# Turning 32 x 128 gather indices: one index load and VectorE squares in place of a column load and a TensorE product

## Chip, cores, metric

One core of one Trainium2 chip. The metric is device time in microseconds (us) of one execution; medians are over several executions, and the ratios compare fast executions with fast ones (an execution counts as slow here when it is over 1.5% above the fastest of the same kernel).

## The reference

```python
def setup_inputs():
    batch, seq, dim = 32, 512, 1024
    x = np.random.randn(batch, seq, dim).astype(np.float32)
    indices = np.random.randint(0, seq, (batch, 128)).astype(np.int32)

def reference(x, indices):          # x [32, 512, 1024], indices [32, 128]
    for b in range(batch):
        result[b] = x[b, indices[b]]   # 128 rows of 4 KB for each batch
```

16.8 MB are written. 15.2 MB of rows are read by the count of the gathers' queue, because from batch 5 on the kernel fetches each distinct row only once. (The page's own line for HBM says 16.81 MB read; why the two differ was not looked into.)

## The kernel before

A gather (indirect transfer, issued by GpSimd) wants one index per partition, so the 32 x 128 table of indices must be turned into 128 x 32. The first five batches (HEAD) are gathered straight into output blocks and stored. For the later 27, VectorE and TensorE first find the distinct rows, GpSimd fetches only these, and TensorE spreads them to the 128 places. Eight buffers (a ring) hold fetched rows. Stores go out on the SyncE queue. The parts that matter here:

```python
first = const.tile([N, 1], indices.dtype, name="first")          # batch 0 as a column
nc.sync.dma_start(out=first[:], in_=indices.rearrange("b n -> n b")[:, 0:1])
vals = const.tile([B, N], indices.dtype, name="vals")            # all indices, by batch
nc.sync.dma_start(out=vals[:], in_=indices)
# ... GpSimd builds small tables: diff, rank (8 pieces), shift ...
dve(v.memset, vf[:], 0.0)
dve(v.tensor_copy, out=vf[:B], in_=<low words of vals>)          # fp16
pe(mm, tr[:], lhsT=vf[:], rhs=ident[:], start=True, stop=True)   # TensorE turns them
dve(v.tensor_copy, out=idxT[:], in_=tr[:])
dve(v.tensor_copy, out=idxF[:], in_=tr[:])
# ... near likewise, from tr ...
for b in range(HEAD):
    gather(blocks[b], first[:].bitcast(I32)[:, 0:1] if b == 0 else idxT[:, b:b + 1], b)
    store(b)
# ... grouping, fetching and spreading of batches 5 to 31 ...
```

Of the kernel before, what the change touches and what calls it, by code (L numbers as in the profile page):

```python
# [6 lines left out]
F32 = mybir.dt.float32  # L7
F16 = mybir.dt.float16
I32 = mybir.dt.int32
ALU = mybir.AluOpType  # L10
# [18 lines left out]
def kernel(ctx, tc, x, indices, out):  # L29
# [14 lines left out]
    nc = tc.nc  # L44
    B, S, D = x.shape
    N = indices.shape[1]
    HEAD, RING, FAR = 5, 8, 1024
    assert S <= FAR
    const = ctx.enter_context(tc.tile_pool(name="const", bufs=1))
# [6 lines left out]
    psm = ctx.enter_context(tc.tile_pool(name="psm", bufs=1, space=PS))  # L56
    pout = ctx.enter_context(tc.tile_pool(name="pout", bufs=3, space=PS))
    pe, dve = InOrder(tc), InOrder(tc)
    mm, v = nc.tensor.matmul, nc.vector


    first = const.tile([N, 1], indices.dtype, name="first")
    nc.sync.dma_start(out=first[:], in_=indices.rearrange("b n -> n b")[:, 0:1])
    vals = const.tile([B, N], indices.dtype, name="vals")
    nc.sync.dma_start(out=vals[:], in_=indices)

# [4 lines left out]
    for e in range(8):  # L71
# [11 lines left out]
    ident = const.tile([N, B], F16, name="ident")  # L83
# [6 lines left out]
    dve(v.tensor_copy, out=turn[:], in_=rank[:].rearrange("p e q -> p (e q)"))  # L90
    vf = const.tile([N, N], F16, name="vf")
    dve(v.memset, vf[:], 0.0)
    dve(v.tensor_copy, out=vf[:B],
        in_=vals[:].bitcast(I32).rearrange("p (n two) -> p n two", two=2)[:, :, 0])


    tr = psm.tile([N, B], F32, name="pos")
    pe(mm, tr[:], lhsT=vf[:], rhs=ident[:], start=True, stop=True)
    idxT = const.tile([N, B], I32, name="idxT")
    dve(v.tensor_copy, out=idxT[:], in_=tr[:])  # L100
    idxF = const.tile([N, B], F32, name="idxF")
    dve(v.tensor_copy, out=idxF[:], in_=tr[:])
    near = const.tile([N, B], F16, name="near")
    dve(v.tensor_scalar, out=near[:], in0=tr[:], scalar1=float(-FAR), scalar2=None, op0=ALU.add)

    xf = x.flatten_outer_dims()
    of = out.flatten_outer_dims()
# [1 line left out]
    def gather(dst, at, b, **kw):  # L109
        nc.gpsimd.indirect_dma_start(  # L110
            out=dst[:], out_offset=None,
            in_=xf[:], in_offset=bass.IndirectOffsetOnAxis(ap=at, axis=0),
            element_offset=b * S * D, **kw)

    def store(b):
        nc.sync.dma_start(out=of[b * N:(b + 1) * N], in_=blocks[b][:])

    blocks = [rows.tile([N, D], F32, name=f"block{b}") for b in range(B)]
    for b in range(HEAD):
        gather(blocks[b], first[:].bitcast(I32)[:, 0:1] if b == 0 else idxT[:, b:b + 1], b)  # L120
        store(b)

    def table(name, dtype):
# [148 lines left out]
```

## Time and profile before

| | before |
|---|---|
| median of the first three executions | 89.02 us (88.86 to 89.25) |
| span of the profiled execution | 87.5 us (that execution: 89.52 us, slower than the median) |
| bytes moved in the whole run | 32.11 MB |
| transfer rate on the plateau, 12 to 84 us | 418 GB/s |
| first gather issued | 2.79 us |
| second gather issued | 4.68 us |

The page cuts the span in 40 slices. The "GB/s" row says how fast transfers moved in each, and it is the row to read first: it is flat at about 418 from slice 7 on, and only the start (the ramp) is lower. The timeline has one line for each instruction: start, length, engine, source line, operation, output<-input, and in brackets how long the engine had been idle and what ended that. The lines themselves stand in the prediction.

### The profile page before, as it was taken

The numbers are of one execution on the slowest core, as the hardware profiler recorded it, in microseconds if no ns is written. First come the engines' busy times: TensorE is split into PE (matmuls) and PEld (weight loads), VectorE is DVE, ScalarE is ACT, GpSimd is POOL, SyncE is SP. The second block draws the span as 40 slices with busy tenths as digits, with TensorE's granted clock in tenths as the row PEclk, the third lists the DMA queues.
The fourth block names the chain that finished last, engine by engine and source line by source line (L and its number), as shares of the span: only waits on it lengthen the run. The fifth ranks groups of instructions, "written<-read, shape, count | busy, mean of one in ns | idle before, by whom it ended". The sixth has DMA issues, their size and how long they took to land.

```text
span 87.5 us, 931 instructions
## 1 busy us (share of the span) xinstructions
PE 58.3 (67%) x184; PEld 23.8 (27%) x184; DVE 41.8 (48%) x265; ACT 40.5 (46%) x63; POOL 33.6 (38%) x46
## 2 busy tenths in 40 slices
PE   0141302006999999999999999998878888885000
PEld 0121101003334343434343433333333332221000
DVE  2399944520497979797979797862000000000000
ACT  6999400000365655555565655554544445555000
POOL 7677787780054545454544444444400000000000
PEclk9999999999999999999999999999999999999995
DMA  0088999999999999999999999999999999999960
GB/s 0 15 223 200 257 352 403 419 419 419 419 416 418 419 421 419 418 418 418 419 414 418 418 412 419 418 418 419 418 419 419 418 419 419 419 419 419 419 251 6
DMA packets 9413, 32.11 MB, mean 367 GB/s; under 512 B 1559, under 2 KB 1591, under 8 KB 9408
## 3 DMA queue, kind: packets, MB, share of 16 engines
q1 hardware_dynamic: 4800, 16.81, 47.2%
q0 software_dynamic: 4608, 15.24, 45.5%
q14 instruction: 4, 0.03, 0.1%
q8 instruction: 1, 0.02, 0.1%
HBM read 16.81 MB, written 16.78 MB: 384 GB/s over the span
## 4 chain that ended last, share of the span: by engine, by line
PE 29%; DVE 29%; DMA 22%; issue 5%; another core or an unknown queue 4%; POOL 1%; ACT 1%; SPq 0%; POOLq 0%; DVEq 0%
PE ps L24 25%; DMA u<-in_x_dram,at 19%; DVE junk L24 5%; DVE s L24 3%; DVE pack L24 3%; DVE s L207 3%; DMA vals<-in_indices_dram 3%; DVE junk L188 3%; DVE lead L24 2%; DVE nth L24 2%; PE pos L24 2%; DVE slot L24 2%; DVE pack L200 1%; DVE atF L204 1%
## 5 line engine op out<-in xcount | busy, mean ns | idle before, releaser
L24 PE MATMUL ps<-u,s 128*128 128x512 f32 x108 | 53.9, 626 | 3.6 <-DMA u<-in_x_dram,at 3.6
L226 ACT COPY block<-ps 128x512 f32<-128x512 f32 x54 | 31.6, 585 | 39.4 <-PE ps L24 31.1
L110 POOL DMA_INDIRECT u<-in_x_dram,at x27 | 26.9, 997 | 26.2 <-PE rk L24 13.0
L24 PEld LDWEIGHTS ps<-u,s 128*128 128x128 f32 x108 | 18.8, 194 | 29.1 <-issue 16.0
L24 DVE SCALAR_TENSOR_TENSOR junk<-bc,idxF,below 128x128 f16<-128x128 f32 x18 | 6.3, 350 | 3.3 <-PE rk L24 3.3
L218 ACT COPY u<-zero 128x1024 f32<-128x1024 f32 x8 | 7.7, 1040 | 0.0
L24 DVE TENSOR_SCALAR s<-bc,atF 128x128 f32<-128x128 f32 x18 | 6.3, 351 | 0.6
L24 PE MATMUL rk<-lead,above 128*128 128x1 f16 x18 | 2.9, 163 | 5.2 <-DVE junk L24 5.2
L24 DVE TENSOR_SCALAR lead<-cnt 128x1 f16<-128x1 f32 (+1 forms) x36 | 3.9, 150 | 4.6 <-remote 4.1
L24 DVE TENSOR_SCALAR pack<-turn,slot,lead 128x128 f16<-128x128 f16 x18 | 5.7, 315 | 0.7
L202 PE MATMUL pos<-near,pack 128*128 128x1 f16 x9 | 1.4, 181 | 5.9 <-DVE pack L200 4.3
L110 POOL DMA_INDIRECT block<-in_x_dram,idxT x4 | 3.8, 946 | 1.7 <-issue 0.9
L24 PEld LDWEIGHTS <-pack 128*128 128x128 f16 x18 | 1.7, 96 | 9.2 <-DVE pack L24 8.8
L24 PE MATMUL bc<-vf,ident 128*128 128x128 f16 x18 | 3.9, 227 | 0.0
L24 PE MATMUL pos<-near,pack 128*128 128x1 f16 x18 | 3.1, 172 | 0.9
L202 PEld LDWEIGHTS <-pack 128*128 128x128 f16 x9 | 0.8, 104 | 9.0 <-DVE pack L200 4.4
L200 DVE TENSOR_SCALAR pack<-turn,slot,lead 128x128 f16<-128x128 f16 x9 | 2.3, 320 | 2.0 <-remote 2.0
L24 DVE TENSOR_TENSOR nth<-nth,shift 128x1 int32<-128x1 int32 x18 | 2.9, 159 | 0.6
L24 DVE CAST slot<-nth 128x1 f32<-128x1 int32 x18 | 2.8, 154 | 0.6
L24 DVE TENSOR_SCALAR at<-pos 128x1 int32<-128x1 f32 x18 | 2.7, 149 | 0.8 <-PE pos L24 0.5
L207 DVE TENSOR_SCALAR s<-bc,atF 128x128 f32<-128x128 f32 x9 | 2.6, 345 | 0.9 <-DVE atF L204 0.9
L188 DVE SCALAR_TENSOR_TENSOR junk<-bc,idxF,below 128x128 f16<-128x128 f32 x9 | 3.0, 345 | 0.0
(37 smaller groups left out, 24.0 us busy)
## 6 DMA issues: line engine op xcount, KB each, us to landing
out_dram<-block SPq DMA_DIRECT2D x32, 512.0 KB
u<-in_x_dram,at POOLq DMA_INDIRECT x27
block<-in_x_dram,idxT POOLq DMA_INDIRECT x4
vals<-in_indices_dram SPq DMA_DIRECT2D x1, 32.0 KB
first<-in_indices_dram SPq DMA_DIRECT2D x1, 1.0 KB
block<-in_x_dram,first POOLq DMA_INDIRECT x1
```

The costliest lines, as they stand in the source:

```text
L24: self.last = do(*args, **kw)
L110: nc.gpsimd.indirect_dma_start(out=dst[:], out_offset=None, in_=xf[:], in_offset=bass.IndirectOffsetOnAxis(ap=at, axis=0), element_offset= ...
L188: v.scalar_tensor_tensor(out=junk[:], in0=bc[:, b - g0], scalar=idxF[:, col(b)], in1=below[:], op0=ALU.is_equal, op1=ALU.mult, accum_out=c ...
L200: v.tensor_scalar(out=pack[:], in0=turn[:], scalar1=slot[:, col(b)], scalar2=lead[:, col(b)], op0=ALU.is_equal, op1=ALU.mult)
L202: pe.last = mm(pos[:, b - g0:b - g0 + 1], lhsT=pack[:], rhs=near[:, col(b)], start=True, stop=True)
L204: v.tensor_scalar(out=t[:, w], in0=pos[:, :n], scalar1=float(FAR), scalar2=None, op0=ALU.add)
L207: dve.last = v.tensor_scalar(out=s[:], in0=bc[:, b - g0], scalar1=atF[:, col(b)], scalar2=None, op0=ALU.is_equal)
L218: nc.scalar.copy(out=u[:], in_=zero[:].to_broadcast([N, D]))
L226: nc.scalar.copy(out=blocks[b][:, w], in_=ps[:])
```

## The change

Its intent: load the indices once only, and let VectorE turn them in four squares of 32 x 32. The small column load with its 128 packets goes, so does the TensorE product. The price is that gather 0 no longer has indices of its own and must wait for the turned ones.

```diff
-    first = const.tile([N, 1], indices.dtype, name="first")
-    nc.sync.dma_start(out=first[:], in_=indices.rearrange("b n -> n b")[:, 0:1])
     vals = const.tile([B, N], indices.dtype, name="vals")
     nc.sync.dma_start(out=vals[:], in_=indices)
 ...
-    dve(v.tensor_copy, out=vf[:B],
-        in_=vals[:].bitcast(I32).rearrange("p (n two) -> p n two", two=2)[:, :, 0])
-    tr = psm.tile([N, B], F32, name="pos")
-    pe(mm, tr[:], lhsT=vf[:], rhs=ident[:], start=True, stop=True)
+    low = vals[:].bitcast(I32).rearrange("p (n two) -> p n two", two=2)[:, :, 0]
     idxT = const.tile([N, B], I32, name="idxT")
-    dve(v.tensor_copy, out=idxT[:], in_=tr[:])
+    for n in range(0, N, B):
+        dve(v.transpose, out=idxT[n:n + B], in_=low[:, n:n + B])
+    dve(v.tensor_copy, out=vf[:B], in_=low)
 ... (idxF and near now read idxT instead of tr)
-        gather(blocks[b], first[:].bitcast(I32)[:, 0:1] if b == 0 else idxT[:, b:b + 1], b)
+        gather(blocks[b], idxT[:, b:b + 1], b)
```

More of the change, by code (lines that the diff above doesn't have):

```diff
@@ L92 @@
     dve(v.memset, vf[:], 0.0)
-    dve(v.tensor_copy, out=vf[:B],
-        in_=vals[:].bitcast(I32).rearrange("p (n two) -> p n two", two=2)[:, :, 0])
-    tr = psm.tile([N, B], F32, name="pos")
-    pe(mm, tr[:], lhsT=vf[:], rhs=ident[:], start=True, stop=True)
+    low = vals[:].bitcast(I32).rearrange("p (n two) -> p n two", two=2)[:, :, 0]
     idxT = const.tile([N, B], I32, name="idxT")
-    dve(v.tensor_copy, out=idxT[:], in_=tr[:])
+    for n in range(0, N, B):
+        dve(v.transpose, out=idxT[n:n + B], in_=low[:, n:n + B])
+    dve(v.tensor_copy, out=vf[:B], in_=low)
     idxF = const.tile([N, B], F32, name="idxF")
-    dve(v.tensor_copy, out=idxF[:], in_=tr[:])
+    dve(v.tensor_copy, out=idxF[:], in_=idxT[:])
     near = const.tile([N, B], F16, name="near")
-    dve(v.tensor_scalar, out=near[:], in0=tr[:], scalar1=float(-FAR), scalar2=None, op0=ALU.add)
+    dve(v.tensor_scalar, out=near[:], in0=idxT[:], scalar1=float(-FAR), scalar2=None, op0=ALU.add)
     xf = x.flatten_outer_dims()
```

## The prediction

> **What bounds the kernel now.** I read the page first: the busy shares, the 40 slices, the DMA queues. Busiest of the engines is TensorE, and none is full; the DMA rows decide it.
>
> ```profile
> PE 58.3 (67%) x184; PEld 23.8 (27%) x184; DVE 41.8 (48%) x265; ACT 40.5 (46%) x63; POOL 33.6 (38%) x46
> ...
> DMA  0088999999999999999999999999999999999960
> GB/s 0 15 223 200 257 352 403 419 419 419 419 416 418 419 421 419 418 418 418 419 414 418 418 412 419 418 418 419 418 419 419 418 419 419 419 419 419 419 251 6
> ...
> HBM read 16.81 MB, written 16.78 MB: 384 GB/s over the span
> ```
>
> One slice is 87.5 / 40 = 2.19 us. From slice 7 (15 us) to slice 38 (83 us) the transfers run at 412 to 421 GB/s without a gap: a plateau, and the kernel is bound by bytes. Only the ramp in slices 1 to 6 is below it. The DMA view of the window from 12 to 84 us says how flat the plateau is:
>
> ```profile
> DMA packets 8667, 30.06 MB, mean 418 GB/s; under 512 B 1336, under 2 KB 1336, under 8 KB 8662
> ```
>
> So 32.11 - 30.06 = about 2 MB of the run's 32.11 MB moves outside these 72 us, some 1.8 MB of it before 12 us. Everything after the ramp is a matter of bytes over 418 GB/s, and the change alters hardly any bytes. What the change can move is the ramp. The chain of waits names TensorE at 29% and VectorE at 29%; I set it aside for the end time, because TensorE's matmuls repeat every 2.07 us a batch (two batches in the 4.13 us from 24.02 to 28.16 us of the chain), whereas a batch's bytes, about 27 gathers' share of (15.24 - 5 x 0.524) / 27 = 0.467 MB plus a store of 0.524 MB, need 0.991 / 0.418 = 2.37 us. TensorE runs ahead and then waits for transfers.
>
> Next the timeline from 0 to 22 us, for GpSimd (start, length, instruction, idle time before it):
>
> ```profile
> 2.27 0.15 POOL L78 IOTA shift<- 128x32 int32 x1
> 2.79 1.11 POOL L110 DMA_INDIRECT block<-in_x_dram,first  x1 [0.37 <-DMA first<-in_indices_dram]
> 4.68 0.95 POOL L110 DMA_INDIRECT block<-in_x_dram,idxT  x1 [0.79 <-DVE idxF L24]
> 5.93 0.95 POOL L110 DMA_INDIRECT block<-in_x_dram,idxT  x1 [0.30 <-issue]
> ```
>
> The gathers are issued one after another, 0.95 to 1.00 us each and 0.30 us between. From the second to the thirteenth (18.80 us) none waits for data by more than this. So the start of the second gather fixes the twelve that fill the ramp; the first stands alone, 1.89 us ahead of it. Now what these two starts wait for, in the same timeline:
>
> ```profile
> 0.74 0.38 SPq L63 DMA_DIRECT2D first<-in_indices_dram  x1
> 1.18 0.41 SPq L65 DMA_DIRECT2D vals<-in_indices_dram  x1
> ...
> 2.52 0.11 DVE L24 MEMSET vf<- 128x64 uint32 x1
> ...
> 3.64 0.27 DVE L24 CAST vf<-vals 32x128 f16<-32x128 int32 x1 [1.00 <-DMA vals<-in_indices_dram]
> ...
> 3.97 0.21 PE L21 MATMUL pos<-ident,vf 128*128 128x32 f16 x1 [3.97 <-DVE vf L24]
> ...
> 4.21 0.19 DVE L24 CAST idxT<-pos 128x32 int32<-128x32 f32 x1 [0.30 <-PE pos L21]
> 4.32 0.18 DVE L24 COPY idxF<-pos 128x32 f32<-128x32 f32 x1
> ```
>
> The wide index load is issued second and lands at 3.54 us (the chain gives it 2.36 us from 1.18). Then cast, product, copy: 3.64 to 4.40 us. GpSimd starts 0.28 us after.
>
> **What the skill says.** "VectorE: DVE Perf Modes", section "The three transpose paths": VectorE turns blocks of 32x32 only. This is why the 32x128 indices need four instructions. The trace of before has no such instruction. The same page, "Two Vector instructions with no wait between them": an instruction whose output starts in another quadrant of 32 partitions than the last one's is held until all earlier ones have finished. The four squares go to four quadrants, so three of them should be held. In before, 128x32 operations last 0.18 to 0.19 us and unheld ones start 0.10 to 0.11 us apart (idxT, idxF), so holding would double their cost. "DMA: Bandwidth & Descriptors", section "Anatomy of one DMA — SWDGE (gpsimd) path": about 2.0 us are fixed, however few the bytes. It agrees in size: vals, 32 KB, takes 2.36 us to land. The same page, "Specifications", puts the fabric ceiling at 435 GB/s; the plateau of 418 lies just under it, so there is no reserve to catch up a late start.
>
> **The change, part by part.**
> - Removed: the column load `first`. It had let gather 0 start at 2.79 us. It was issued before vals, so vals now goes out at 0.74 instead of 1.18, 0.44 us earlier. Its 128 tiny packets are no bytes to speak of.
> - Removed from the path to idxT: cast (0.33 us to the product's start), product and its wait (0.24), copy (0.19): 3.64 to 4.40, 0.76 us.
> - Added to it: four squares. Unheld: 3 x 0.10 + 0.19 = 0.49 us; held: 4 x 0.19 = 0.76 us, or 0.95 if a square costs 0.24. I choose 0.70.
> - Start of the squares: with the old latency vals is ready at 3.64 - 0.44 = 3.20 us. If it was slow only because it queued behind `first`, it could be ready when the memset ends, 2.63 us. I choose 3.05.
> - Moved: cast of vf now comes after the squares; products for the comparisons start about 4.0 us as before, idxF and near come from SBUF. VectorE's rank work starts within 0.3 us of its old 4.62. It has slack: `at` of the first group is written at 7.77 and first used at 9.68 us.
>
> Sum: idxT at 3.05 + 0.70 = 3.75, gather 0 at 4.03 us, which is 1.24 later than 2.79. The first gather took 1.11 us against 0.95 for the next; I let it stay so, and gather 1 starts at 4.03 + 1.11 + 0.30 = 5.44, which is 0.76 later than 4.68. All gathers up to the thirteenth move by that. The order of instructions in the changed kernel confirms it: five gathers by idxT in a row, the first waiting for VectorE.
>
> To the end: if the whole ramp moves by 0.76 us, so does the end. If the slow part of the ramp ends at a fixed time (the rate reaches 401 GB/s at 12 us, just when VectorE's first burst ends at 11.96), the loss is the bytes moved in the last 0.76 us before, about 0.76 x 300 GB/s = 0.23 MB, over 418 = 0.55 us. I take **+0.6 us**: 89.02 + 0.6 = 89.6 us.
>
> **The rivals.**
> - *An index path that is quicker than the old one.* vals ready at 2.65 and unheld squares 0.49: idxT at 3.14, gather 0 at 3.42, gather 1 at 4.83, only 0.15 later than before. Then 89.0 to 89.2. For it: the packets of vals move mostly from 2.2 to 2.6 us, and only a last trace of 10 GB/s at 3.2 to 3.3 us keeps it from landing. Against: that straggler may come again.
> - *A slow path.* Squares of 0.24 us held, strided source, vals at 3.20: gather 1 1.16 us later, 90.1. Also, idxF and near now read SBUF while GpSimd writes the first descriptors, and might hold it for some tenths.
> - *The ramp is hidden anyway.* Gather 0 moved slowly and alone (its store could be issued only at 7.48 us), so bunching it with gather 1 may lose nothing, and the end moves by 0.3 or less. Against: a plateau with no reserve never repays a late byte.
> - *TensorE becomes the bound.* Its first spreading product at 20.44 us follows a VectorE stall of 1.7 to 2.3 us which the profile gives to an unknown queue. By 20 us thirteen gathers and five stores (8.9 MB) are asked for and some 5.2 MB moved, so 3.7 MB or 9 us of transfers are waiting: a stall would have to grow by many us. Unlikely.
>
> **Range and chances.** The paths above give +0.0 to +1.1 us; runs of before spread by 0.2 us either way. So 88.9 to 90.3 should hold it 8 times in 10. The lines for 2% are 87.2 and 90.8 us. Faster needs something outside this account, as no part of the path to the end shrinks by 1.8 us: 1%. Slower needs a delay of 1.8 us in the ramp or a transfer gap: 4%. Within: 95%.
>
> **What would show it.** Right: the plateau stays at 418 GB/s; vals issued at 0.74 and landed by 3.1; four squares of about 0.2 us; the first gather about 4.0 and the second about 5.4 us, then 1.25 to 1.30 apart; the first store near 8.5 instead of 7.48; the end about 0.6 later. Wrong in its steps: vals landing still at 3.5 (issue order bought nothing), squares far from 0.2 us, or a second gather later than 0.76 with an end that does not move. Wrong altogether: the plateau changes rate, or a gap opens in it.

## The result

The changed kernel is slightly slower: 90.12 us median (89.68 to 90.38, 4 executions) against 88.95 (88.86 to 89.25, 4 executions). The ratio is 1.0121, 95% interval 1.0071 to 1.017. A ratio here is the mean time of one kernel's fast runs over that of the other's fast runs of the same rounds, so it is not quite the ratio of the medians. Two more measurements followed (below): 1.005 (1.0016 to 1.0083) and 1.0111 (1.0064 to 1.0158). The mean of the three ratios is 1.0094, which is 0.0094 x 89.0 = 0.84 us. This is real, but under the 2% line, and inside the predicted range.

The page of the changed kernel, the rows of transfers in 40 slices of 2.2 us:

```profile
DMA  0048879999999999999999999999999999999950
GB/s 15 0 85 309 297 244 420 418 416 418 420 418 422 420 418 416 418 415 422 416 413 407 416 416 422 418 420 420 416 418 420 416 418 416 420 424 416 424 229 7
```

The plateau is the same as before (about 418 GB/s); the ramp is what differs. Here is what the ramp starts with, from the timeline of SyncE's queue, of VectorE and of GpSimd:

```profile
0.74 0.39 SPq L63 DMA_DIRECT2D vals<-in_indices_dram  x1
...
2.52 0.11 DVE L24 MEMSET vf<- 128x64 uint32 x1
2.55 0.79 DVE L24 STREAM_TRANSPOSE idxT<-vals 32x32 int32<-32x32 int32 x4
3.37 0.21 DVE L24 CAST vf<-vals 32x128 f16<-32x128 int32 x1
3.52 0.16 DVE L24 CAST idxF<-idxT 128x32 f32<-128x32 int32 x1
...
3.62 1.11 POOL L107 DMA_INDIRECT block<-in_x_dram,idxT  x1 [1.20 <-DVE vf L24]
5.04 0.95 POOL L107 DMA_INDIRECT block<-in_x_dram,idxT  x1 [0.31 <-issue]
6.29 0.94 POOL L107 DMA_INDIRECT block<-in_x_dram,idxT  x1 [0.30 <-issue]
```

The squares start as soon as VectorE is free, take 0.79 us together, and the first gather is issued at 3.62 instead of 2.79 us (+0.83), the second at 5.04 instead of 4.68 (+0.36). The bracket at the first gather names "DVE vf", an instruction that started at 3.37, when the last square had ended; the indices that it needs are those of the squares.

Now the same stretch as bytes. Each line below is one microsecond; the last two columns are the busy share of the 16 DMA engines and the rate in GB/s. Before:

```profile
6.00:7.00 1.00, 0.00 (x0) 0.00 (x0) 1.00 (x10) 1.00 (x2) 0.88 (x1) 1.00 1.03 274
7.00:8.00 1.00, 0.42 (x3) 0.29 (x4) 1.00 (x9) 1.00 (x2) 0.82 (x1) 1.00 0.53 119
8.00:9.00 1.00, 0.00 (x0) 0.00 (x0) 1.00 (x7) 1.00 (x2) 0.69 (x2) 1.00 1.09 311
9.00:10.00 1.00, 0.50 (x4) 0.25 (x3) 1.00 (x7) 0.69 (x1) 0.70 (x2) 1.00 0.93 291
10.00:11.00 1.00, 0.33 (x2) 0.17 (x2) 0.79 (x7) 0.00 (x0) 0.69 (x2) 1.00 0.94 221
11.00:12.00 1.00, 0.00 (x0) 0.00 (x0) 0.96 (x5) 0.00 (x0) 0.99 (x1) 1.00 0.86 291
12.00:13.00 1.00, 0.00 (x0) 0.00 (x0) 0.00 (x0) 0.00 (x0) 0.71 (x1) 1.00 1.01 414
```

Changed:

```profile
6.00:7.00 1.00, 0.28 (x3) 0.20 (x4) 1.00 (x10) 1.00 (x2) 0.71 (x1) 1.00 0.76 283
7.00:8.00 1.00, 0.15 (x2) 0.09 (x3) 1.00 (x9) 1.00 (x2) 0.70 (x2) 1.00 0.89 270
8.00:9.00 1.00, 0.23 (x2) 0.07 (x1) 1.00 (x9) 1.00 (x2) 0.69 (x2) 1.00 0.83 303
9.00:10.00 1.00, 0.67 (x4) 0.34 (x4) 0.76 (x4) 0.69 (x1) 0.74 (x1) 1.00 1.04 348
10.00:11.00 1.00, 0.00 (x0) 0.00 (x0) 0.97 (x6) 0.00 (x0) 0.96 (x1) 1.00 0.68 238
11.00:12.00 1.00, 0.09 (x1) 0.10 (x1) 0.96 (x6) 0.00 (x0) 0.70 (x2) 1.00 0.56 123
12.00:13.00 1.00, 0.71 (x5) 0.38 (x6) 0.68 (x5) 0.00 (x0) 0.70 (x2) 1.00 0.88 319
```

One microsecond at 1 GB/s is 0.001 MB, so the last column sums directly. In this pair of profiles the changed kernel moves 1.20 MB against 1.00 MB from 6 to 10 us, the mean rate from 0 to 10 us is 132 GB/s in both, and it falls behind between 11 and 13 us, where it moves 0.44 MB against 0.71. But the two are level at 10 us only because the profile of before has a late second gather (4.68 us). Three kernels that take as long as before and issue it at 4.18 to 4.31 us (column load with squares, short gap, stores exchanged; all below) had moved 1.50 to 1.57 MB by 10 us in their profiles; the changed kernel had moved 1.30 to 1.32 MB in its three. Against these the debt is there by 10 us already. By 16 us the pair shows a debt too. The DMA view of the first 16 us, before and then changed:

```profile
DMA packets 1116, 3.47 MB, mean 217 GB/s; under 512 B 246, under 2 KB 278, under 8 KB 1115
```

```profile
DMA packets 915, 3.26 MB, mean 204 GB/s; under 512 B 96, under 2 KB 128, under 8 KB 914
```

The debt is 0.21 MB; at 418 GB/s that is 0.5 us, and the plateau never repays it. The spans of the two profiles differ by 0.6 us (88.1 and 87.5).

### The profile page after: what moved, and what is told of

It is laid out like the page before. It is cut to its first block, busy times and chain, and to the rows that moved or that the text cites. A ratio compares the mean times of both kernels' runs of the same rounds, so it can differ in the third digit from the quotient of the medians.

```text
span 88.1 us, 929 instructions
## 1 busy us (share of the span) xinstructions
PE 59.1 (67%) x183; PEld 24.3 (28%) x183; DVE 42.4 (48%) x268; ACT 40.6 (46%) x63; POOL 33.6 (38%) x46
## 4 chain that ended last, share of the span: by engine, by line
DMA 47%; PE 19%; DVE 16%; issue 6%; POOL 3%; ACT 1%; POOLq 0%
DMA u<-in_x_dram,at 47%; PE ps L24 17%; DVE junk L24 2%; DVE junk L185 2%; DVE s L24 2%; DVE pack L24 2%; POOL block L107 2%; POOL rank L74 1%; DVE nth L24 1%; DVE lead L24 1%; DVE slot L24 1%; PE pos L24 1%; DVE idxT L24 1%; ACT block L223 1%; DVE lead L188 1%
## 5 line engine op out<-in xcount | busy, mean ns | idle before, releaser
L24 DVE TENSOR_SCALAR s<-bc,atF 128x128 f32<-128x128 f32 x18 | 6.3, 351 | 0.6
L24 DVE TENSOR_SCALAR pack<-turn,slot,lead 128x128 f16<-128x128 f16 x18 | 5.7, 314 | 0.7
L107 POOL DMA_INDIRECT block<-in_x_dram,idxT x5 | 4.9, 979 | 2.4 <-DVE vf L24 1.2
L24 PE MATMUL bc<-vf,ident 128*128 128x128 f16 x18 | 3.9, 227 | 0.0
L182 PE MATMUL bc<-vf,ident 128*128 128x128 f16 x9 | 1.1, 309 | 3.6 <-DVE vf L24 3.6
L24 PEld LDWEIGHTS <-ident 128*128 128x128 f16 x18 | 1.8, 102 | 4.1 <-issue 4.1
```

The costliest lines, as they stand in the source:

```text
L24: self.last = do(*args, **kw)
L107: nc.gpsimd.indirect_dma_start(out=dst[:], out_offset=None, in_=xf[:], in_offset=bass.IndirectOffsetOnAxis(ap=at, axis=0), element_offset= ...
L182: mm(bc[:, b - g0], lhsT=ident[:, col(b)].to_broadcast([N, N]), rhs=vf[:], start=True, stop=True)
```

## The experiments

Three theories went in. **Second gather:** the end follows the start of the second gather and of the train behind it. **First gather:** the end follows the first gather, since the gathers' queue is then busy for so long that the second has time to spare. **Squares:** the VectorE path itself costs. Later came **first store:** the ramp is slow because only gathers run, and ends when stores begin. In the table, "MB by 16 us" and the issue times are from one profile of each kernel, the ratio from five rounds against the kernel before; the first row is the one profile that this document has of the kernel before. The medians take in slow executions where there were some (one each of "gather 0 later" and "store 1 ahead", three of the last row); the ratios do not.

| kernel | first, second gather issued (us) | MB by 16 us | median us | ratio (95% interval) |
|---|---|---|---|---|
| before | 2.79, 4.68 | 3.47 | 89.0 to 89.15 | 1 |
| changed, second measurement | 3.63, 5.04 | 3.19 | 89.65 | 1.005 (1.0016 to 1.0083) |
| changed, third measurement | 3.78, 5.21 | 3.26 | 89.88 | 1.0111 (1.0064 to 1.0158) |
| squares, column load kept | 2.76, 4.18 | 3.66 | 89.10 | 0.9987 (0.9952 to 1.0023) |
| product, column load gone | 3.66, 5.07 | 3.27 | 89.92 | 1.0074 (1.004 to 1.0108) |
| before, long gap behind gather 0 | 2.76, 6.29 | 3.07 | 90.27 | 1.0144 (1.0108 to 1.0179) |
| before, short gap | 2.76, 4.31 | 3.52 | 89.13 | 0.9994 (0.9947 to 1.0042) |
| before, middle gap | 2.76, 4.74 | 3.45 | 89.40 | 1.0032 (0.9988 to 1.0076) |
| before, gather 0 a little late | 3.10, 4.52 | 3.55 | 89.21 | 1.0039 (0.9992 to 1.0086) |
| before, gather 0 later | 3.94, 5.38 | 3.14 | 90.26 | 1.0103 (1.0053 to 1.0153) |
| before, store 1 ahead of store 0 | 2.83, 4.31 | 3.45 | 89.28 | 1.0016 (0.9962 to 1.007) |
| before, gather 0 in two halves | 3.30, 4.67 (the halves) | 3.05 | 90.07 | 1.0107 (1.0051 to 1.0163) |
| column, squares, tables later | 2.76, 4.16 | 3.38 | 90.05 | 1.0041 (0.9996 to 1.0085) |

Read downward: the kernels with 3.27 MB or less by 16 us have ratios of 1.005 to 1.0144, those with 3.38 MB or more 0.9987 to 1.0041. One profile stands beside several timed executions, so this is a regularity over twelve kernels, not a law for one.

### The change again, as a yardstick

No edit. 

> The changed kernel itself, beside the kernel before in five rounds on one chip, as the yardstick for the other runs. The first measurement gave a ratio of 1.012 with an interval of 1.007 to 1.017; I expect 1.008 to 1.015, the first gather issued at 3.6 us and the second at 5.0.

Measured 1.005; a third time:

> The changed kernel once more, as the yardstick of this call: the first two measurements gave ratios of 1.012 and 1.005, whose intervals meet at 1.007 to 1.008. I expect 1.004 to 1.011.

Measured 1.0111. The squares start at 2.55 or 2.65 us, the first gather at 3.63 or 3.78. The size of the loss is thus known as 0.5 to 1.2% and no better.

### Undo one half: column load back, squares kept

```diff
 (changed kernel)
+    first = const.tile([N, 1], indices.dtype, name="first")
+    nc.sync.dma_start(out=first[:], in_=indices.rearrange("b n -> n b")[:, 0:1])
     vals = ...
-        gather(blocks[b], idxT[:, b:b + 1], b)
+        gather(blocks[b], first[:].bitcast(I32)[:, 0:1] if b == 0 else idxT[:, b:b + 1], b)
```

> The squares stay, the column load of batch 0 comes back ahead of the wide load, so that the first gather is again issued at 2.79 us. Theory 'first gather or first store' (what the change costs is the later first gather): back to the kernel before, ratio 0.998 to 1.003. Theory 'second gather' (the end follows the start of the second gather and the train behind it; with the wide load again second, the squares end at 4.4 us or so, second gather near 4.7 as before): also about 1.000. Theory 'squares' (the VectorE path itself costs, by locks or order): stays near 1.010.

Measured 0.9987. The loss is gone, with all four squares still there. "Squares" falls: VectorE's squares cost nothing at the end of the kernel. They gain nothing either, though 3.66 MB by 16 us is the best of all; the interval of the time includes 1. The squares had to wait for vals, which landed 1.67 us after its issue although the column load was ahead of it (before: 2.36 us):

```profile
2.88 0.85 DVE L24 STREAM_TRANSPOSE idxT<-vals 32x32 int32<-32x32 int32 x4 [0.24 <-DMA vals<-in_indices_dram]
```

### Undo the other half: product kept, column load gone

```diff
 (kernel before)
-    first = const.tile([N, 1], indices.dtype, name="first")
-    nc.sync.dma_start(out=first[:], in_=indices.rearrange("b n -> n b")[:, 0:1])
-        gather(blocks[b], first[:].bitcast(I32)[:, 0:1] if b == 0 else idxT[:, b:b + 1], b)
+        gather(blocks[b], idxT[:, b:b + 1], b)
```

> The column load is taken away, TensorE still turns the indices. The wide load lands at 2.5 us, cast, product and copy take 0.76, the first gather is issued at about 3.6 us, the second 1.41 later. Theory 'first gather or first store': like the changed kernel, ratio 1.008 to 1.015. Theory 'second gather' (+0.3 us): 1.003 to 1.004. Theory 'squares': 1.000.

Measured 1.0074, with the start of the gathers almost that of the changed kernel:

```profile
3.66 1.11 POOL L108 DMA_INDIRECT block<-in_x_dram,idxT  x1 [1.24 <-DVE idxF L24]
5.07 0.95 POOL L108 DMA_INDIRECT block<-in_x_dram,idxT  x1 [0.30 <-issue]
```

With the run above this settles which part of the change costs: taking away the column load does, and how the indices are turned does not. The intervals of the two runs do not touch.

### Move the second gather alone: a long gap

```diff
 (kernel before)
+    idle = const.tile([N, 1700], I32, name="idle")
+    pool = InOrder(tc)
     for b in range(HEAD):
+        if b == 1:
+            pool(nc.gpsimd.iota, idle[:], pattern=[[1, 1700]], base=0, channel_multiplier=0)
-        gather(...)
+        pool(gather, ...)
```

> The kernel before, with one dummy GpSimd operation of about 1 us between the first and the second gather: the first stays at 2.79 us, the second and all behind it start 0.3 to 0.6 us later. Theory 'second gather': the end moves by as much, ratio 1.003 to 1.007. Theory 'first gather': [...]a second gather issued at 5.1 us has 0.3 us to spare or so and the ratio stays 0.998 to 1.002.

Measured 1.0144, and not for either reason: the dummy was longer than meant (1.56 us), and VectorE's cast was held as well. Timeline of GpSimd and VectorE:

```profile
3.88 1.56 POOL L24 IOTA idle<- 128x1700 int32 x1
6.29 0.95 POOL L110 DMA_INDIRECT block<-in_x_dram,idxT  x1 [0.85 <-DVE idxF L24]
...
3.24 2.28 DVE L24 CAST vf<-vals 32x128 f16<-32x128 int32 x1 [0.60 <-DMA vals<-in_indices_dram]
```

The cast of 0.2 to 0.3 us lasted 2.28 us and ended at 5.52, 0.08 after the dummy. The Trainium skill says this: "SBUF — State Buffer", section "SBUF: two separate sides", calls the port pair that VectorE and GpSimd share "an **exclusive lock**, not a bandwidth split"; whichever starts first holds it for its whole instruction. The end of the cast fits that, but not its start: the cast began at 3.24 us, 0.64 us before the dummy and while the first gather (2.76 to 3.86 us) was being issued. In the run with the middle gap a cast begun at 3.07 ended at 3.87 us, just behind that gather, while in others it took 0.21 us beside one; so what held it first is not shown. The late cast made the second gather come at 6.29 us, and the transfers ran dry:

```profile
7.00:8.00 1.00, 0.16 (x1) 0.00 (x0) 1.00 (x11) 1.00 (x2) 0.69 (x2) 1.00 0.17 16
8.00:9.00 1.00, 0.12 (x1) 0.10 (x1) 1.00 (x8) 1.00 (x2) 0.69 (x2) 1.00 0.89 70
```

What follows is this much: with the first gather in its place, a second that is 1.6 us later than in the profile of before costs 0.0144 x 89.0 = 1.3 us. A late second gather does cost, once it is late enough.

### Shorter gaps

As above, with 128 and with 650 in place of 1700.

> As the run with a gap after the first gather, but with a dummy of 0.2 us instead of the 1.56 us that it turned out to be, so that the second gather is issued near 5.0 us, where the changed kernel issues it, while the first stays at 2.8. Theory 'second gather': +0.3 us, ratio 1.003 to 1.005. Theory 'first gather'[...]: nothing, 0.998 to 1.002.

Measured 0.9994. This run missed its aim: the second gather was issued at 4.31 us, which is where the run with the stores exchanged has it without any dummy. The wide index load had landed earlier than in the profile of before (the cast after it started at 3.33 instead of 3.64 us), and the dummy fitted into the wait. It tells nothing of a delay.

> The kernel before with a dummy of about 0.75 us between the first and the second gather: first at 2.8 us, second at 4.8 to 5.0 instead of 4.3 to 4.7, about where the changed kernel has it. Theory 'second gather': the loss of the changed kernel comes back, ratio 1.005 to 1.008. Theory 'first gather': the gathers' queue still has rows of the first one to move until 6.7 us, nothing is lost, 0.998 to 1.003.

Measured 1.0032 with an interval of 0.9988 to 1.0076, the second gather at 4.74 us. That is 0.06 us from the profile of before, though 0.43 from 4.31; the changed kernel's 5.04 to 5.21 was not reached. Between the two theories this is inconclusive.

### Delay the first gather, both loads and the product kept

```diff
 (kernel before, ahead of the first gather; 500 and 1500 columns)
+    idle = const.tile([N, 500], I32, name="idle")
+    pool = InOrder(tc)
+    pool(nc.gpsimd.iota, idle[:], pattern=[[1, 500]], base=0, channel_multiplier=0)
```

> The kernel before, column load and product and all, with a dummy GpSimd operation of about 0.5 us ahead of the first gather, which is then issued at 3.3 to 3.8 us instead of 2.8; VectorE's path is untouched. Theory 'first gather': the whole loss of the changed kernel comes back, ratio 1.005 to 1.012, and bytes moved by 16 us fall short of before by 0.15 to 0.25 MB. Theory 'squares': 1.000.

Measured 1.0039 (0.9992 to 1.0086): the dummy gave a delay of 0.31 us only, 3.10 us, and the effect is not clear of noise. The larger dose:

> The kernel before with a dummy of about 1.5 us ahead of the first gather, issued then near 4.2 us instead of 2.8 (the smaller dummy, +0.3 us, gave a ratio of 1.004 with an interval of 0.999 to 1.009). Theory 'first gather': +1.0 to +1.5 us, ratio 1.011 to 1.017. If the ramp hides late starts: under 1.006.

Measured 1.0103 (1.0053 to 1.0153), with the first gather at 3.94 (+1.15) and the second at 5.38 (+0.70 on the profile of before): 0.92 us for 1.15 us of delay. The loss of the changed kernel comes back without any square or any missing product. The index path was not quite untouched, though: VectorE's cast ahead of it was held until the dummy (2.39 to 3.76 us) had ended.

```profile
2.33 1.50 DVE L24 CAST turn<-rank 128x128 f16<-128x128 int32 x1 [0.79 <-POOL rank L76]
...
3.94 1.14 POOL L113 DMA_INDIRECT block<-in_x_dram,first  x1 [0.19 <-issue]
```

This made idxT start at 4.39 instead of 4.21 us. It was still ready ahead of the second gather, and up to the thirteenth gather none was idle for more than 0.30 us before it, so what was late in the ramp were the gathers. But this dummy moves both gathers, so it does not say which of the two counts.

### Move the first store

```diff
 (kernel before)
     for b in range(HEAD):
         gather(...)
-        store(b)
+    sp = InOrder(tc)
+    for b in (1, 0, 2, 3, 4):
+        sp(store, b)
```

> The kernel before, with the store of block 1 asked for ahead of that of block 0 on the same queue: no gather moves, but the first store can be issued only when the second gather has landed, about 9.8 us instead of 7.5. Theory 'first store' (the ramp is slow because only the gathers' queue works, and ends when stores begin): the end moves by 0.5 to 1 us, ratio 1.006 to 1.012. Theory 'first gather alone' (the train of gathers decides, stores only fill in): 0.998 to 1.003.

Measured 1.0016 (0.9962 to 1.007). The first store was issued 2.35 us later than before (9.83 instead of 7.48 us, SyncE's queue):

```profile
9.83 0.36 SPq L116 DMA_DIRECT2D out_dram<-block  x1
```

and still 3.45 MB had moved by 16 us. "First store" in the strong form falls: when stores begin late, the gathers use the time.

### Two attempts at a faster version

Gather 0 and its store in halves of 64 rows, so that storing can begin earlier:

```diff
 (kernel before)
-    first = const.tile([N, 1], ...); load of column 0
+    first = const.tile([64, 2], ...); load of indices[0] as 64 x 2
+        if b == 0:
+            for h in range(2):
+                half = slice(h * 64, (h + 1) * 64)
+                gather(blocks[b][half], first[:].bitcast(I32)[:, 2 * h:2 * h + 1], b)
+                nc.sync.dma_start(out=of[half], in_=blocks[b][half])
+            continue
```

> The kernel before, with the first gather and its store in two halves of 64 rows, so that the first store can be issued about 1 us earlier (6.4 instead of 7.5). Theory 'first store': faster, by 0.3 to 0.6 us, ratio 0.993 to 0.997. Theory 'first gather alone': 0.999 to 1.002, or slower if two small gathers cost GpSimd more than one.

Measured 1.0107, slower. Half a gather costs GpSimd nearly as much as a whole one, the column in this form landed later, at about 3.3 us, and the first store was issued at 7.32 us, hardly earlier than 7.48 (6.4 was meant):

```profile
3.30 1.06 POOL L110 DMA_INDIRECT block<-in_x_dram,first  x1 [0.88 <-DMA first<-in_indices_dram]
4.67 0.92 POOL L110 DMA_INDIRECT block<-in_x_dram,first  x1 [0.30 <-issue]
5.89 0.96 POOL L110 DMA_INDIRECT block<-in_x_dram,idxT  x1 [0.30 <-DVE lead L197]
```

The gather of batch 1 is issued at 5.89 us. It is one more case of late gathers.

Column load and squares, with GpSimd's tables moved behind the second gather:

```diff
 (squares with the column load)
-    rank = ...; 8 x nc.gpsimd.iota(rank...); shift = ...; nc.gpsimd.iota(shift...)   # ahead of gather 0
+    # the same nine, issued in order between gather 1 and gather 2; turn is made from rank later
```

> A version meant to beat both: column load and squares, and GpSimd's nine small tables for the ranking moved from ahead of the first gather to behind the second, so that the first gather is issued as soon as the column lands, about 2.4 us instead of 2.8. Theory 'first gather': 0.2 to 0.4 us faster than before, ratio 0.995 to 0.999. It could lose if the third gather, now some 1.4 us later, leaves the gathers' queue empty, or the tables come late for the ranking.

Measured 1.0041 (0.9996 to 1.0085), no gain. This ratio rests on three executions; the other three count as slow by their time, though their granted clock was not lower (0.986 to 0.988 against 0.982 to 0.983), so a loss is not ruled out. The profile is one of the slow ones, so I take only the start times from it:

```profile
2.76 1.09 POOL L96 DMA_INDIRECT block<-in_x_dram,first  x1 [1.70 <-DMA first<-in_indices_dram]
```

With GpSimd idle for 1.70 us the first gather still starts at 2.76: it waits for the column to land, not for the tables. The third gather went from 5.43 to 6.69 us instead. So no version tried beats the kernel before.

## Why the prediction was right or wrong

- **What bounds the kernel, and that the plateau repays nothing:** right. The plateau is at 418 GB/s in both kernels, and 0.21 MB less by 16 us agrees with the 0.6 us between the spans.
- **The landing of vals:** mis-sized. It was taken as ready for the squares at 3.05 us; it landed 1.7 us after its issue, about 2.4 us, before VectorE was free. Of the rivals, the quicker index path was right in this step. Queueing behind the column load is at most a part of the reason: six later profiles with both loads have a landing 1.67 to 2.05 us after the issue, so the 2.36 us on which the estimate stood was a slow draw.
- **The squares:** 0.70 us chosen, 0.79 to 0.85 measured, about 0.2 us each and one after another, as "VectorE: DVE Perf Modes", section "Two Vector instructions with no wait between them", says of outputs in different quadrants.
- **The gathers:** predicted at 4.03 and 5.44 us, measured 3.62 and 5.04, both 0.4 early because of vals. The first gather kept its 1.11 us, the spacing its 1.25.
- **"All gathers up to the thirteenth move by that, so does the end":** the weak step. By the profiles the second gather moved by 0.36 us and the kernel lost 0.84 (mean of three). One reason is the reference: 4.68 us in the one profile of before is a slow draw. In later runs with the same two loads and the product the cast after the wide load started at 3.07 to 3.33 instead of 3.64, and the second gather, where nothing held it, at 4.31. Against 4.31 the second gather moved by 0.73. That is close to the predicted 0.76, but two errors cancelled.
- **The first gather** was said to stand alone ahead of the train, which fixes the ramp. Whether its 0.83 us or the train's delay makes the loss is open: no run delayed the first gather alone, nor the second to 5.0 to 5.2 us alone. Shown is that late gathers as such make it (+1.15 and +0.70 us give 0.92), and that the path by squares does not. The record leans to the train. Sorted by the gather of batch 1, the ratios rise nearly in step: 0.9987 at 4.18 us, 0.9994 and 1.0016 at 4.31, 1.0039 at 4.52, 1.0032 at 4.74, 1.005 to 1.0121 at 5.04 to 5.21, 1.0103 at 5.38, 1.0107 at 5.89, 1.0144 at 6.29 (left out: the last row, in which it is the third gather that is late). Sorted by the first gather they do not: the greatest loss has it at 2.76 us. With one profile to a kernel this is a regularity, not a proof.
- **That bunching hides part of the late start:** it seemed so in the first pair of profiles, with equal bytes by 10 us and the debt at 11 to 13 us. Against the profiles with a second gather at 4.18 to 4.31 us some 0.2 MB were missing by 10 us already, so no hiding is shown. Why the rate sinks to 123 GB/s at 11 to 12 us is not settled. Late stores are not enough of a reason, as the exchanged stores show.
- **The first store** was expected near 8.5 us and came at 8.28. **TensorE as the bound:** did not come about.
- **Time:** 89.6 predicted, 90.12 in the first measurement, 89.65 and 89.88 in the next two. Direction, size under 2% and range held; the loss of 0.6 us was slightly small.

## What to carry to other kernels

Where transfers are the bound and run without reserve, look at what starts the first of them: a tiny extra load that lets the first large transfer go 0.8 us earlier is worth its instruction, even if another load brings the same data. Test the halves of a change apart: here one half was free and the other cost all. Do not size a delay of some tenths of a microsecond against one profile; the landing of a small load alone moved by 0.3 to 0.7 us between runs.

## What the Trainium skill lacked or had wrong

- "DMA: Bandwidth & Descriptors", section "Specifications", gives an HBM limit of about 358 GB/s for one core, and does not say beside the figure that this is the share of a core whose neighbour is busy too, as the skill does elsewhere. On this one core, reads from HBM and writes to it together ran, counted by packets, at 364 to 367 GB/s in the mean over the whole run and at 418 on the plateau, for 72 us; the fabric ceiling of 435 in the same table fits.
- The same page, section "Anatomy of one DMA — SWDGE (gpsimd) path", gives a fixed cost of about 2.0 us plus size, for transfers that GpSimd issues. On SyncE's queue a load of 32 KB landed in 1.7 us alone and, behind the column load, in 1.67 to 2.05 us in six profiles and in 2.36 in one; how far a small load's landing moves from run to run is not told there.
- No page that I read tells what an indirect gather costs GpSimd by its rows: 1.06 and 0.92 us for 64 rows, 1.11 and 0.95 us for 128. The cost is nearly all that of the instruction, not of its rows; and the first one of a run took 0.14 to 0.19 us more.
- "VectorE: DVE Perf Modes", section "The three transpose paths", has a time for 128x128 only. A 32x32 square of int32, read with a stride of two words, took 0.14 to 0.20 us, and four into four quadrants 0.79 to 0.85 us.
